# Attention of a hybrid diffusion trunk: score matmuls of two heads in row halves of the array, values stationary in column halves

## The chip, the cores and the metric

One NeuronCore of a Trainium2 chip runs the whole program in one launch. The metric is device time in microseconds (us) from start to end of an execution. Five engines work from queues of their own, each in order: TensorE (PE in the rows, its weight loads PEld), VectorE (DVE), ScalarE (ACT), GpSimd (POOL) and SyncE (SP, which issues most DMAs). They wait for each other through semaphores.

## The reference, cut to what matters

Two layers of a trunk run over 128 context tokens ("ctx") and 512 latent tokens ("lat"). Each layer has a token mixer of three branches (gated linear attention, a short convolution, windowed attention) and a feed-forward part that gathers experts. The change is in the windowed attention alone:

```python
qb = q.reshape(B, nb, ATT_BLOCK, ATT_KV_HEADS, ATT_GROUP, hd)      # 16 heads of 64, 4 key heads
s_loc = jnp.einsum('bnqhgd,bnkhd->bnhgqk', qb, kb) * scale          # 3 key blocks of 128 around each query block
s_loc = jnp.where(valid, s_loc, -jnp.inf)
s_ctx = jnp.einsum('bnqhgd,bchd->bnhgqc', qb, kc) * scale           # 128 cached context keys
m = max(max(s_loc), max(s_ctx), sink)
p_loc, p_ctx = jnp.exp(s_loc - m), jnp.exp(s_ctx - m)
den = sum(p_loc) + sum(p_ctx) + jnp.exp(sink - m)
o = einsum('bnhgqk,bnkhd->bnqhgd', p_loc / den, vb) + einsum('bnhgqc,bchd->bnqhgd', p_ctx / den, vc)
```

Context attention is the same with one block of 128 keys and no mask.

## The kernel before, in words

`attn` works on pairs of heads. A feature tile `ft` (8 per layer) holds two query heads, 64 features each, on the 128 partitions: `qH`, and for the latent tokens `qL`, the rest that the rounded `qH` leaves. Keys are stored the same way, two key heads (`h` = 0, 1) on 128 partitions, but once for each of the two heads with the other head's 64 rows set to zero by `half` (`k_split`, tile `km`, results `kH`, `kL`). So one score matmul contracts over all 128 rows and sees one head. A latent score is three matmuls (`mm3`, lines 198 to 200: H by H, H by L, L by H) into a PSUM tile `S` of the kind `pb` (two buffers) with 3 or 4 blocks of 128 keys, and one or two mask matmuls (L688).

For each block `j` of 128 queries and each head: largest score (L690), its scaled negative `nm` (L691), exponential with row sum (L694) into `P`, transposes of `P` on TensorE (L698) into a `pt` tile, a copy to `PT` (head 0 on DVE, L703; head 1 on ACT, L701, as the flag `FL[0]` is 0), then `P` times `V` (L706) with `PT` as the stationary operand and 64 value columns moving, into `po` with the queries on partitions. After four blocks the sums are inverted, `po` is multiplied by them (L715), and four transposes (L719) turn the tile back to features on partitions; ACT copies it and a DMA stores it (L722).

An fp32 matmul (operands `F32`, as `P`, `V`, the context's scores) is two rows in the trace, an fp32r one (`F32R`, as `qH`, `kH`) or a transpose is one.

Other work shares the queues. In the latent mixer `attn` is a background generator that is advanced while the convolution's projections run (L198 to L200 into `pa`), and the expert gather (POOL fetches, DVE multiplies `gjunk`, `gacc`) advances beside both. In the context mixer it runs beside the merge (L365) and the modulation (L269). A scheduler decides from this at which place in each engine's order an instruction stands.

Two kinds of matmul before the change already use only a part of the array: the modulation (L269) puts 32 weight columns in one of four column groups, and the decay projection (L410) 16 rows at row 0 or row 32.

Of the kernel before, what the change touches and what calls it, by code (L numbers as in the profile page):

```python
# [43 lines left out]
def kernel(ctx: ExitStack, tc: tile.TileContext, A: dict, O: list):  # L44
# [327 lines left out]
    def flat(x):  # L372
        return x.rearrange("p s t -> p (s t)")
# [213 lines left out]
    def attn(s, l, hH, hL, ap):  # L587

        if True:
# [8 lines left out]
            kH = [[t4k([128, nk, 128], "kH%d%d" % (i, h), kt_, s, ap) for h in range(2)] for i in range(2)]  # L598
            kL = [[None if s.ctx else ap.tile([128, nk, 128], F32R, name="kL%d%d" % (i, h), bufs=1)
                   for h in range(2)] for i in range(2)]  # L600

            def k_split(i, pos, x):
                n = x.shape[-1]
# [52 lines left out]
            for un in range(4):  # L656
                ps = proj_fm(s, hH, hL, w_for(s, A["w_in"][l, 24 + un]))
                for f in range(2):
# [12 lines left out]
                    po = po2([128, 2, nq, 64])  # L671
                    for j in range(nq):
# [6 lines left out]
                        n = len(poss)  # L679
                        for h in range(2):  # L680
                            qs = slice(j * 128, (j + 1) * 128)
                            S = pb([128, n, 128])
                            ks = slice(poss[0], poss[0] + n)
                            k2 = lambda x: None if x is None else flat(x[pr][h][:, ks, :])
                            mm3(flat(S), qH[:, qs], None if s.ctx else qL[:, qs], k2(kH),
                                None if s.ctx else k2(kL), True, not masks)
                            for mi, (i, w) in enumerate(masks):
                                nc.tensor.matmul(S[:, i, :], idb, band[:, w, :], start=False, stop=mi == len(masks) - 1)  # L688
                            mx = ap.tile([128, 1], F32, name="mx", bufs=4)
                            V.reduce_max(mx, flat(S), axis=mybir.AxisListType.X)  # L690
                            V.scalar_tensor_tensor(nm[:, j, h:h + 1], mx, -ASCALE, nsink[:, ft, h:h + 1],  # L691
                                                   op0=OP.mult, op1=OP.min)
                            P = ap.tile([128, n, 128], F32, name="P", bufs=2)
                            act(flat(P), flat(S), AF.Exp, scale=ASCALE, bias=nm[:, j, h:h + 1],  # L694
                                accum_out=den[:, j, h:h + 1])
                            ptp = pt([128, n, 128])
                            for i in range(n):
                                nc.tensor.transpose(ptp[:, i, :], P[:, i, :], idf)  # L698
                            PT = ap.tile([128, n, 128], F32, name="PT", bufs=2)
# [18 lines left out]
                    for j in range(nq):  # L718
                        nc.tensor.transpose(p[:, j, :], y[:, j].rearrange("p h d -> p (h d)"), idf)  # L719
# [794 lines left out]
```

## Time and profile before

| | us |
|---|---|
| runs before: median (lowest to highest of 3) | 5597.84 (5595.0 to 5608.46) |
| the profiled execution's own time | 5604.7 |
| its span, first to last instruction | 5602.9 |
| TensorE busy | 5117.3 |
| VectorE busy | 4190.2 |
| ScalarE busy | 2014.7 |
| GpSimd busy | 2482.5 |

Busy times overlap. A busy TensorE is counted from a matmul's start to its modelled end; matmuls are pipelined, so the distance between the starts of two neighbours tells what one costs, not its length. Context attention lies at about 223 to 310 us and 1780 to 1895 us, latent attention at about 720 to 1026 us (layer 0) and 3505 to 3865 us (layer 1).

### The profile page before, as it was taken

To read this page: it belongs to the slowest core of one execution; us is meant where nothing else is said; L and a number is where in the kernel's file an instruction comes from. 1 tells how busy PE (TensorE), PEld (TensorE's weight loads), DVE (VectorE), ACT (ScalarE), POOL (GpSimd) and SP (SyncE) were. 2 spreads that over 40 slices of the span, in tenths; PEclk is the share of its full clock that TensorE was granted. 3 is DMA by queue.
4 is the path that set the end of the run, shared out by engine and by line. 5 is a ranking of instruction groups with operands and counts; after the bars stand their busy time and mean duration, and the time that the engine had idled before them with its cause. 6 is when DMAs were issued, how large, how long until landed. Compare 5 with 4: busy or idle time off the path is not lost. (4 is left out here: it accounts for less than half of the span.)

```text
span 5602.9 us, 78403 instructions
## 1 busy us (share of the span) xinstructions
PE 5117.3 (91%) x28598; PEld 4457.9 (80%) x28598; DVE 4190.2 (75%) x7436; ACT 2014.7 (36%) x3454; POOL 2482.5 (44%) x1907
## 2 busy tenths in 40 slices
PE   8999889988899999899999798998998899999998
PEld 6888777767688998888777587777776899899876
DVE  3328978877544868887777789788878986788777
ACT  2214434221232225653333344333223367333333
POOL 1112434676210006886555543455753254665432
PEclk9999999999899999999999899999998999999999
DMA  7773456887566667899999634578852574999996
GB/s 297 272 246 127 136 185 223 303 297 250 208 222 235 226 233 267 323 337 325 322 314 323 214 123 139 194 257 288 286 187 101 191 260 175 359 324 322 328 327 214
DMA packets 456707, 1395.08 MB, mean 249 GB/s; under 512 B 42880, under 2 KB 184832, under 8 KB 413312
## 3 DMA queue, kind: packets, MB, share of 16 engines
q1 hardware_dynamic: 303248, 833.73, 42.1%
q0 software_dynamic: 153072, 556.34, 28.7%
q8 instruction: 225, 3.69, 0.3%
q14 instruction: 162, 1.33, 0.1%
HBM read 1275.29 MB, written 114.62 MB: 248 GB/s over the span
## 5 line engine op out<-in xcount | busy, mean ns | idle before, releaser
L917 POOL DMA_INDIRECT grow<-in_peer_u_dram,eidx x512 | 696.0, 1359 | 635.6 <-DVE gjunk L922 257.4
L917 POOL DMA_INDIRECT grow<-in_peer_v_dram,eidx x512 | 671.9, 1312 | 553.2 <-DVE gacc L934 248.4
L934 DVE SCALAR_TENSOR_TENSOR gacc<-grow,gw,gacc 128x1024 f32<-128x1024 f32 x508 | 707.0, 1392 | 86.8 <-DMA grow<-in_peer_v_dram,eidx 80.4
L178 POOL TENSOR_TENSOR wl<-wraw,wh 128x640 fp32r<-128x640 f32 (+1 forms) x260 | 413.4, 1592 | 720.5 <-ACT wh L174 659.4
L922 DVE SCALAR_TENSOR_TENSOR gjunk<-grow,gh 128x1024 bf16<-128x1024 f32 x512 | 682.0, 1332 | 67.1 <-DMA grow<-in_peer_u_dram,eidx 62.6
L174 ACT ACTIVATE wh<-wraw 128x1024 fp32r<-128x1024 f32 (+1 forms) x388 | 515.7, 1343 | 520.7 <-PE pa L199 207.3
L176 DVE TENSOR_TENSOR wl<-wraw,wh 128x1408 fp32r<-128x1408 f32 (+2 forms) x388 | 557.5, 1440 | 150.5 <-ACT wh L174 148.2
L198 PE MATMUL acc<-wh,daH 128*128 128x512 f32 x1536 | 611.2, 399 | 51.9 <-ACT daH L112 37.5
L200 PE MATMUL acc<-wh,daL 128*128 128x512 f32 x1536 | 610.7, 398 | 13.8 <-DVE daL L113 13.4
L199 PE MATMUL acc<-wl,daH 128*128 128x512 f32 x1536 | 607.3, 395 | 0.5 <-DVE wl L176 0.5
L198 PE MATMUL pa<-hH,wh 128*128 128x512 f32 x1312 | 542.5, 414 | 43.6 <-DVE th L744 11.2
L200 PE MATMUL pa<-hH,wl 128*128 128x512 f32 x1312 | 535.6, 410 | 9.0 <-DVE wl L176 8.8
L199 PE MATMUL pa<-hL,wh 128*128 128x512 f32 x1312 | 534.8, 408 | 0.5 <-DVE hL L113 0.4
L198 PE MATMUL po<-hH,uH 128*128 128x384 f32 x1376 | 484.3, 352 | 20.6 <-ACT uH L1014 14.0
L200 PE MATMUL po<-hH,uL 128*128 128x384 f32 x1376 | 471.6, 343 | 9.6 <-DVE uL L1016 9.3
L199 PE MATMUL po<-hL,uH 128*128 128x384 f32 x1376 | 470.5, 342 | 0.0
L1014 ACT ACTIVATE uH<-uraw 128x1024 fp32r<-128x1024 f32 x256 | 270.7, 1058 | 555.6 <-PE po L199 223.3
L198 PEld LDWEIGHTS acc<-wh,daH 128*128 128x128 f32 x1536 | 294.4, 192 | 121.7 <-ACT daH L112 47.8
L987 POOL TENSOR_SCALAR ob<-iota,tt,tt 128x128 f32<-128x128 f32 x192 | 292.4, 1528 | 211.0 <-ACT tt L968 91.3
L1016 DVE TENSOR_TENSOR uL<-uraw,uH 128x1024 fp32r<-128x1024 f32 (+1 forms) x256 | 284.4, 1111 | 119.9 <-ACT uH L1014 118.8
L200 PEld LDWEIGHTS acc<-wh,daL 128*128 128x128 f32 x1536 | 293.8, 191 | 91.0 <-DVE daL L113 29.6
L198 PEld LDWEIGHTS pa<-hH,wh 128*128 128x128 f32 x1312 | 255.0, 195 | 110.5 <-DVE th L744 12.9
(367 smaller groups left out, 11610.7 us busy)
## 6 DMA issues: line engine op xcount, KB each, us to landing
wraw<-in_w_in_dram SPq DMA_DIRECT2D x168, 1024.0 KB
uraw<-in_u_T_dram SPq DMA_DIRECT2D x256, 512.0 KB
wraw<-in_v_n_dram SPq DMA_DIRECT2D x256, 512.0 KB
wraw<-in_w_mod_dram SPq DMA_DIRECT2D x48, 1024.0 KB
wraw<-in_w_branch_dram SPq DMA_DIRECT2D x48, 1024.0 KB
gdr<-stage SPq DMA_DIRECT2D x24, 2048.0 KB
G<-gdr SPq DMA_DIRECT2D x64, 768.0 KB
sdr<-ust SPq DMA_DIRECT2D x172, 192.0 KB
```

What stands on the lines that cost most here:

```text
L174: act(H, raw, AF.Copy)
L176: V.tensor_sub(L[:, :m], raw[:, :m], H[:, :m].bitcast(F32))
L178: nc.gpsimd.tensor_sub(L[:, m:], raw[:, m:], H[:, m:].bitcast(F32))
L198: nc.tensor.matmul(out, aH, bH, start=start, stop=False)
L199: nc.tensor.matmul(out, aH, bL, start=False, stop=False)
L200: nc.tensor.matmul(out, aL, bH, start=False, stop=stop)
L917: nc.gpsimd.indirect_dma_start(out=g, out_offset=None, in_=A[tab + str(l)], in_offset=bass.IndirectOffsetOnAxis(ap=eidx[:, j:j + 1], axis=0))
L922: pin(V.scalar_tensor_tensor(junk, g, 1.0, h, op0=OP.mult, op1=OP.mult, accum_out=w[:, j:j + 1]))
L934: pin(V.scalar_tensor_tensor(acc, g, w[:, j:j + 1], acc, op0=OP.mult, op1=OP.add))
L987: (nc.gpsimd if w == "P" else V).tensor_scalar(ob[:, k, :], iota128, TT[1][:, j:j + 1], TT[2][:, j:j + 1], op0=OP.is_equal, op1=OP.mult)
L1014: act(uH, raw, AF.Copy)
L1016: V.tensor_sub(uL[:, :m, :], raw[:, :m, :], uH[:, :m, :].bitcast(F32))
```

## The change

Scores: keys are stored once (no zeroed halves), and each head's score matmul contracts over its own 64 rows, at row 0 or row 64 of the array (`tile_position=(64 * h, 0)`). The two heads' matmuls are issued in turn, into the two `pb` buffers. One `nm` operation serves both heads. Values: `V` (64 columns) is now stationary, in the left or right column half of the array (`tile_position=(0, 64 * h)`), `PT` moves with 128 columns, and `po` comes out with features on partitions. So the closing transposes are gone; instead the reciprocal sums are spread over 64 partitions each by a matmul with the identity (L724 of the changed kernel), copied by ACT to `rd`, and multiplied in. Both heads' `PT` are copied by ACT. The generator yields after the exponentials of both heads and after both heads' `P` times `V`, as many times as before.

```diff
-                for h in range(2):
-                    if s.ctx:
-                        V.tensor_scalar(flat(kH[i][h][:, pos, :]), x, half[:, h:h + 1], None, op0=OP.mult)
-                        continue
-                    km = ap.tile([128, 512], F32, tag="km", name="km", bufs=1)
-                    V.tensor_scalar(km[:, :n], x, half[:, h:h + 1], None, op0=OP.mult)
-                    split(flat(kH[i][h][:, pos, :]), flat(kL[i][h][:, pos, :]), km[:, :n])
+                if s.ctx:
+                    act(flat(kH[i][:, pos, :]), x, AF.Copy)
+                else:
+                    split(flat(kH[i][:, pos, :]), flat(kL[i][:, pos, :]), x)
...
+                        S = [pb([128, n, 128]) for _ in range(2)]
+                        terms = [(qH, kH[pr])] if s.ctx else [(qH, kH[pr]), (qH, kL[pr]), (qL, kH[pr])]
+                        for m, (q_, k_) in enumerate(terms):
+                            for h in range(2):
+                                nc.tensor.matmul(flat(S[h]), q_[hs[h], qs], flat(k_[hs[h], ks, :]), start=m == 0,
+                                                 stop=m == len(terms) - 1 and not masks, tile_position=(64 * h, 0))
...
-                            mm3(flat(S), qH[:, qs], None if s.ctx else qL[:, qs], k2(kH),
-                                None if s.ctx else k2(kL), True, not masks)
...
+                        V.scalar_tensor_tensor(nm[:, j, :], mx, -ASCALE, nsink[:, ft, :], op0=OP.mult, op1=OP.min)
...
-                            if h or FL[0]:
-                                act(flat(PT), flat(ptp), AF.Copy)
-                            else:
-                                V.tensor_copy(flat(PT), flat(ptp))
-                            for i in range(n):
+                            act(flat(PT[h]), flat(ptp), AF.Copy)
+
+                        for i in range(n):
+                            for h in range(2):
                                 vs = slice(pr * 128 + h * 64, pr * 128 + h * 64 + 64)
-                                nc.tensor.matmul(po[:, h, j, :], PT[:, i, :], vt[:, poss[i] % 5, vs],
-                                                 start=i == 0 and j == 0 and h == 0, stop=i == n - 1, skip_group_check=True)
-                            yield
+                                nc.tensor.matmul(po[hs[h], j, :], vt[:, poss[i] % 5, vs], PT[h][:, i, :],
+                                                 start=i == 0 and j == 0, stop=i == n - 1, tile_position=(0, 64 * h),
+                                                 skip_group_check=True)
+                        yield
...
-                        nc.tensor.transpose(p[:, j, :], y[:, j].rearrange("p h d -> p (h d)"), idf)
-                    yT = ap.tile([128, nq, 128], F32, name="yatT", bufs=1)
-                    act(flat(yT), flat(p), AF.Copy)
+                        for h in range(2):
+                            nc.tensor.matmul(p[hs[h], j, :], den[:, j, h:h + 1].to_broadcast([128, 64]), idf,
+                                             start=True, stop=True, tile_position=(0, 64 * h), skip_group_check=True)
+                    rd = ap.tile([128, nq, 128], F32, name="rd", bufs=1)
+                    act(flat(rd), flat(p), AF.Copy)
+                    yT = ap.tile([128, nq, 128], F32, name="yatT", bufs=2)
+                    V.tensor_mul(flat(yT), flat(po), flat(rd))
```

First place: TensorE's order in latent attention of layer 0, at the scores of a query block of four key blocks. Before, the scores of the two heads (`kH00`, `kH01`: the same keys with one or the other half zeroed) stand together behind a run of `P` times `V`:

```order
L706 MATMUL po_6574<-vt_5576,PT_6629 128x64 x4
L706 MATMUL po_6574<-vt_5576,PT_6651 128x64 x4
L198 MATMUL pb_6733<-kH01_5569,qH_6560 128x512
L199 MATMUL pb_6711<-kL00_5572,qH_6560 128x512
L199 MATMUL pb_6733<-kL01_5573,qH_6560 128x512
L200 MATMUL pb_6711<-kH00_5568,qL_6561 128x512
L200 MATMUL pb_6733<-kH01_5569,qL_6561 128x512
```

Now (L684, row halves; `pb_6240` is head 0, `pb_6241` head 1) transposes of the previous block's `P` (L704, full array) stand between them:

```order
L704 MATMUL pt_6218<-idf_75,P_6214 128x128
L684 MATMUL pb_6240<-kH0_5556,qH_6106 128x512
L704 MATMUL pt_6218<-idf_75,P_6214 128x128
L684 MATMUL pb_6240<-kL0_5558,qH_6106 128x512
L684 MATMUL pb_6241<-kH0_5556,qH_6106 128x512
L704 MATMUL pt_6218<-idf_75,P_6214 128x128
L684 MATMUL pb_6241<-kL0_5558,qH_6106 128x512
L704 MATMUL pt_6218<-idf_75,P_6214 128x128
L684 MATMUL pb_6240<-kH0_5556,qL_6107 128x512
L684 MATMUL pb_6241<-kH0_5556,qL_6107 128x512
```

What moved: the six score matmuls are as many as before, but full-array and row-half instructions now alternate.

Second place: TensorE's order at `P` times `V` in the same stretch. Before (L706, all on the full array, as the transposes L698 and the scores of the next block are):

```order
L706 MATMUL po<-vt,PT 128x64 x4
L698 MATMUL pt<-idf,P 128x128 x4
L706 MATMUL po<-vt,PT 128x64 x2
L698 MATMUL pt<-idf,P 128x128 x4
L198 MATMUL pb<-kH_5568,qH 128x512
```

Now (L711 and the spreading of the reciprocal sums L724 in column halves; L704, and the convolution's L198 to L200, on the full array):

```order
L711 MATMUL po<-PT,vt 64x128
L198 MATMUL pa<-hH,wh 128x512
L199 MATMUL pa<-hL,wh 128x512
L200 MATMUL pa<-hH,wl 128x512
L711 MATMUL po<-PT,vt 64x128 x7
L704 MATMUL pt<-idf,P 128x128 x3
L198 MATMUL pa<-hH,wh 128x512
L199 MATMUL pa<-hL,wh 128x512
L704 MATMUL pt<-idf,P 128x128 x2
L724 MATMUL pt<-idf,den 64x128 x2
L704 MATMUL pt<-idf,P 128x128
L724 MATMUL pt<-idf,den 64x128 x2
```

What moved: one or two column-half matmuls stand alone between others, seven stand together, and the spreading has come in between.

Third place: VectorE's order in latent attention of layer 0. Before:

```order
L690 TENSOR_REDUCE mx<-pb 128x1 x2
L691 SCALAR_TENSOR_TENSOR nm<-mx,nsink 128x1
L703 COPY PT<-pt 128x384
L691 SCALAR_TENSOR_TENSOR nm<-mx,nsink 128x1
L922 SCALAR_TENSOR_TENSOR gjunk,gw<-grow,gh 128x1024
L703 COPY PT<-pt 128x512
```

Now (`gacc` is a row of the expert gather):

```order
L692 TENSOR_REDUCE mx<-pb 128x1 x2
L942 SCALAR_TENSOR_TENSOR gacc<-grow,gw,gacc 128x1024
L693 SCALAR_TENSOR_TENSOR nm<-mx,nsink 128x2
L582 TENSOR_TENSOR yc<-yc,pa 128x512
L942 SCALAR_TENSOR_TENSOR gacc<-grow,gw,gacc 128x1024
L176 TENSOR_TENSOR wl<-wraw,wh 128x1408
```

What moved: the copies to `PT` are gone from this queue (they are on ACT), and one `nm` of both heads follows both largest scores.

## Rows read from the trace of the kernel before

**Rows 1.** The page, part 1: busy us, share of the span, instructions of each engine.
```profile
PE 5117.3 (91%) x28598; PEld 4457.9 (80%) x28598; DVE 4190.2 (75%) x7436; ACT 2014.7 (36%) x3454; POOL 2482.5 (44%) x1907
```

**Rows 2.** Table by stage: the four attention stretches; then clock, DMA share, GB/s.
```profile
core 0 of [0], span 5602.9 us
...
223.00:310.00 87.00, 85.64 (x669) 76.41 (x670) 23.11 (x93) 19.55 (x82) 16.99 (x17) 1.00 0.85 305
1780.00:1895.00 115.00, 114.69 (x838) 104.51 (x838) 62.68 (x282) 30.19 (x102) 2.98 (x1) 1.00 0.65 226
720.00:1026.00 306.00, 294.86 (x1714) 240.66 (x1713) 260.45 (x432) 122.21 (x241) 137.01 (x116) 0.99 0.65 214
3505.00:3865.00 360.00, 326.94 (x1809) 266.33 (x1807) 299.18 (x481) 130.55 (x251) 176.98 (x144) 0.95 0.69 232
```

**Rows 3.** Groups by line, 720 to 1026 us: busy us, mean ns | idle before.
```profile
L706 PE MATMUL po<-vt,PT 128*128 128x64 f32 x448 | 57.5, 269 | 0.5 <-DVE PT L703 0.4
L706 PEld LDWEIGHTS po<-vt,PT 128*128 128x128 f32 x448 | 56.8, 191 | 5.9 <-ACT PT L701 1.9 <-DVE PT L703 1.4 <-issue 0.5
...
L703 DVE COPY PT<-pt 128x384 f32<-128x384 f32 (+1 forms) x32 | 19.8, 618 | 3.8 <-PE pt L698 3.3 <-PE po L706 0.2
...
L691 DVE SCALAR_TENSOR_TENSOR nm<-mx,nsink 128x1 f32<-128x1 f32 x64 | 14.8, 233 | 0.0
...
L719 PE MATMUL pt<-idf,yat 128*128 128x128 f32 x32 | 4.8, 273 | 0.0
```

**Rows 4.** Timeline, 783 to 805 us: start, us, engine, instruction, count.
```profile
783.24 0.39 PE L199 MATMUL pb<-kL,qH 128*128 128x512 f32 x1
783.47 0.40 PE L200 MATMUL pb<-kH,qL 128*128 128x512 f32 x1
...
784.06 0.75 PEld L706 LDWEIGHTS po<-vt,PT 128*128 128x128 f32 x6
...
795.90 0.34 PE L199 MATMUL pb<-kL,qH 128*128 128x384 f32 x1
796.07 0.34 PE L200 MATMUL pb<-kH,qL 128*128 128x384 f32 x1
...
803.62 0.60 PE L719 MATMUL pt<-idf,yat 128*128 128x128 f32 x4
```

**Rows 5.** Timeline around a change of the array's shape, 232 to 238 us.
```profile
232.83 3.12 PE L365 MATMUL pa<-yH,wraw 128*128 128x128 f32 x26
235.88 0.14 PEld L269 LDWEIGHTS pb<-wraw,cT 128*32 128x32 f32 x2
235.88 0.62 PE L269 MATMUL pb<-wraw,cT 128*32 128x256 f32 x2
...
236.43 0.30 PEld L196 LDWEIGHTS pb<-kH,qH 128*128 128x128 f32 x2 [0.41 <-issue]
...
236.85 0.58 PEld L269 LDWEIGHTS pb<-wraw,cT 128*32 128x32 f32 x14
...
237.84 0.74 PEld L365 LDWEIGHTS pa<-hF,wraw 128*128 128x128 f32 x6 [0.41 <-issue]
```

**Rows 6.** Line L269: durations in ns, least, median, most.
```profile
L269 PE MATMUL pb<-wraw,cT x768: 379/379/637, 8.8 to 1865.0; 128*32 128x256 f32 x192
```

**Rows 7.** Timeline: one 16-row group at 84 us, two at 98 us.
```profile
83.92 0.48 PE L410 MATMUL pb<-gaT,a 16*128 16x128 f32 x2
...
84.34 0.41 PEld L365 LDWEIGHTS pa<-hF,wraw 128*128 128x128 f32 x3
...
97.61 0.49 PE L410 MATMUL pb<-gaT,a 16*128 16x128 f32 x4
...
98.03 0.63 PEld L365 LDWEIGHTS pa<-hF,wraw 128*128 128x128 f32 x5
```

**Rows 8.** Who waited for whom, PE, 3505 to 3865 us: total, times, longest.
```profile
PE pb L198 <- ACT qH L112: 8.2, 3, 5.5
PE pa L200 <- DVE wl L176: 6.8, 3, 4.8
```

More of the change, by code (lines that the diff above doesn't have):

```diff
@@ L597, in attn @@
             kt_ = F32 if s.ctx else F32R
-            kH = [[t4k([128, nk, 128], "kH%d%d" % (i, h), kt_, s, ap) for h in range(2)] for i in range(2)]
-            kL = [[None if s.ctx else ap.tile([128, nk, 128], F32R, name="kL%d%d" % (i, h), bufs=1)
-                   for h in range(2)] for i in range(2)]
+            kH = [t4k([128, nk, 128], "kH%d" % i, kt_, s, ap) for i in range(2)]
+            kL = [None if s.ctx else ap.tile([128, nk, 128], F32R, name="kL%d" % i, bufs=1) for i in range(2)]
             def k_split(i, pos, x):
-                n = x.shape[-1]
-                for h in range(2):
-                    if s.ctx:
-                        V.tensor_scalar(flat(kH[i][h][:, pos, :]), x, half[:, h:h + 1], None, op0=OP.mult)
-                        continue
-                    km = ap.tile([128, 512], F32, tag="km", name="km", bufs=1)
-                    V.tensor_scalar(km[:, :n], x, half[:, h:h + 1], None, op0=OP.mult)
-                    split(flat(kH[i][h][:, pos, :]), flat(kL[i][h][:, pos, :]), km[:, :n])
+                if s.ctx:
+                    act(flat(kH[i][:, pos, :]), x, AF.Copy)
+                else:
+                    split(flat(kH[i][:, pos, :]), flat(kL[i][:, pos, :]), x)
             vt = ap.tile([128, 1 if s.ctx else 5, 256], F32, name="vt", bufs=1)
@@ L679, in attn @@
                         n = len(poss)
-                        for h in range(2):
[L681 to L684, printed above, removed]
-                            mm3(flat(S), qH[:, qs], None if s.ctx else qL[:, qs], k2(kH),
-                                None if s.ctx else k2(kL), True, not masks)
[L687 to L694, printed above, removed]
@@ new lines, in attn @@
+                        qs = slice(j * 128, (j + 1) * 128)
+                        ks = slice(poss[0], poss[0] + n)
+                        hs = [slice(64 * h, 64 * h + 64) for h in range(2)]
+                        S = [pb([128, n, 128]) for _ in range(2)]
[4 more added lines that the diff above has]
+                                                 stop=m == len(terms) - 1 and not masks, tile_position=(64 * h, 0))
@@ new lines, in attn @@
+                        for mi, (i, w) in enumerate(masks):
+                            for h in range(2):
+                                nc.tensor.matmul(S[h][:, i, :], idb, band[:, w, :], start=False,
+                                                 stop=mi == len(masks) - 1)
+                        mx = ap.tile([128, 2], F32, name="mx", bufs=4)
+                        for h in range(2):
+                            V.reduce_max(mx[:, h:h + 1], flat(S[h]), axis=mybir.AxisListType.X)
+                        V.scalar_tensor_tensor(nm[:, j, :], mx, -ASCALE, nsink[:, ft, :], op0=OP.mult, op1=OP.min)
@@ L695, in attn @@
+                        P = []
+                        for h in range(2):
+                            P.append(ap.tile([128, n, 128], F32, name="P", bufs=2))
+                            act(flat(P[h]), flat(S[h]), AF.Exp, scale=ASCALE, bias=nm[:, j, h:h + 1],
                                 accum_out=den[:, j, h:h + 1])
+                        yield
+                        PT = []
+                        for h in range(2):
                             ptp = pt([128, n, 128])
                             for i in range(n):
-                                nc.tensor.transpose(ptp[:, i, :], P[:, i, :], idf)
@@ L709, in attn @@
+                        yield
                     es = ap.tile([128, nq, 2], F32, name="es", bufs=2)
```

10 lines of the change are left out of this document (5 added, 5 removed).

## Prediction

> **What bounds the kernel now.** I read the page first, to see which engine the span is made of. TensorE (PE) has work for 91% of it [rows 1], so the question is whether PE is also what the four attention stretches wait for. The table by stage answers that [rows 2]: context attention (223 to 310 us, 1780 to 1895 us) has PE busy 85.6 of 87 and 114.7 of 115 us; latent attention has it busy 294.9 of 306 us in layer 0 and 326.9 of 360 us in layer 1. VectorE (DVE) stands at 260 of 306 us, ScalarE (ACT) at 122. So in three stretches time is the sum of what PE's queue holds; only in the fourth are there 33 us to fill, and 11 in the second, 44 together. The longest PE waits of that fourth stretch are for qH and wl [rows 8], made by ACT and DVE.
>
> PE executes its queue in order, so I take the change as a sum over PE's instructions, multiplied by distances between neighbours in the trace.
>
> **What the array is given less of.** Per latent layer, before: 192 score matmuls, half of 384 and half of 512 columns, start 0.17 and 0.23 us apart [rows 4], mean 0.20: 38.4 us. 448 rows of P times V (224 matmuls, two rows each [rows 3]), whose weight loads follow each other at (0.75-0.19)/5 = 0.112 us [rows 4] (one lasts 0.19 [rows 3]): 50.2 us. 32 closing transposes at (0.60-0.27)/3 = 0.11 us [rows 4] (one lasts 0.27 [rows 3]): 3.5 us. Together 92.1 us.
>
> Do halves of the array run side by side? The trace of before has both kinds. The modulation matmul (L269) uses four column groups: alone in its group the second row of a pair starts 0.62-0.38 = 0.24 us after the first (0.38 is the length of one [rows 6]), while 14 of them take 237.84-236.85 = 0.99 us, 0.07 each [rows 5]. The decay matmul (L410) uses 16-row groups: from its start to the next weight load of the full array one group's two rows take 84.34-83.92 = 0.42 us, and two groups' four rows 98.03-97.61 = 0.42 us [rows 7]. So I take two halves for the price of one, where the order puts both halves next to each other. It often does not: counted over the order of the changed kernel, 56 of the 192 score matmuls of a latent layer stand without a partner (a transposition of P is between them, as in the first place shown above), so 68+56 = 124 slots of 0.20: 24.8 us. Of 288 column-half matmuls (224 of P times V, 64 that spread the reciprocal sums) 58 have none: 115+58 = 173 slots of two rows at 0.11: 38.1 us. After: 62.9 us, 29.2 less per latent layer. The 224 transposes of P, the masks and the rotary matmuls stay. Context attention, by the same counting with 128-column fp32 scores (0.22 each): 8.1 us before, 7.5 and 7.7 after. All four: 2 x 29.2 + 1.0 = 59.4 us less.
>
> **What it is given more of: changes of the array's shape.** The changed kernel goes from full to row halves to column halves and back. Before, the order has 166 such changes (L269 and L410); after, 915: 749 more, 653 of them in latent attention (342 and 311). Their price is in [rows 5]. The 26 rows of L365 start (3.12-0.27)/25 = 0.114 apart (0.27 as for L706 and L719 [rows 3]); the last starts at 235.68 and has streamed at 235.79, but the first weight load of the column groups begins at 235.88: 0.09 us in which nothing starts. Then L196: from its load (236.43) to the next group's (236.85) are 0.42 us: two streams of 0.114, again 0.09 of standing, and 0.10 in which the array waits for the first 128 columns of weights, which nothing hides. So 0.20 us where full-width fp32 weights or score weights come next (213 to scores, 101 to other full ones, latent; 67 in context): 381 x 0.20 = 76.2. I take 0.15 where 64-column weights or transposes come next (half the load to hide; a choice between 0.09 and 0.20): 136+159 latent, 29 context: 324 x 0.15 = 48.6; 0.12 for 44 masks: 5.3. Sum 130.1 us. Bounds: 749 x 0.09 = 67 and 749 x 0.20 = 150.
>
> Here a rule of the Trainium skill speaks against the change. TensorEngine Tiling (Array Packing), section Key Properties: changing the tiling mode, as against the tile, drains TensorE. It gives no time; if a drain lasted until the recorded end of the last matmul (0.27 us after its start, 0.16 after its stream), a switch would cost 0.07 us more than the rows show and the sum would rise by some 50 us. The rows show 0.09, and I go by them.
>
> **Moved off and onto the other engines.** DVE loses 32 copies of turned probabilities per latent layer (19.8 us [rows 3]) and half of 64 small scalings of 0.233 us (7.4 us), besides the masked key halves: some 30 of 260 busy us. ACT takes the copies (about the same 0.6 us each): 122 to about 142 of 306 us, still far from full. The cover for ACT is PE's bound. The closing multiply stays one DVE operation per tile, and one PSUM copy on ACT remains. What the lighter DVE gives is that waits of PE for DVE's products shrink: of 44 us of PE idle [rows 2] I take 10; bounds 0 and 44. The number of DMAs is unchanged: the same one store per feature tile.
>
> **Sum.** 130.1 - 59.4 - 10 = +60.7 us. The profiled execution took 5604.7 us (span 5602.9 [rows 2]), so 5665; it stands 6.9 us over the median of the runs (5597.84), in whose terms I forecast **5658 us**.
>
> **Rivals.**
> - *The switch is free* (ends on the other side). If what the halves load is fetched while the full array still streams, 749 changes cost nothing and 59.4 us are gained: 5538 us. It decides at 59.4/749 = 0.079 us a switch: below that the kernel is faster. Against it: [rows 5] shows 0.09 of standing three times in a row, before any weight. For it: those are 32-wide groups, and no row shows 64-wide ones. 7%. The Trainium skill (TensorE: Matmul & The Clock Gate, Part 3, The mechanism) has weight loads pulled ahead of running matmuls where row groups differ; a half and the full array share theirs.
> - *PE's idle time swallows it.* If a lighter DVE and a busier PE use up all 44 us, +27 remain: 5625. For it: the waits in [rows 8] are for DVE's and ACT's work. Against: in layer 0 there are only 11 us to use, and ACT's products are as late as before. 15%.
> - *The halves do not overlap* (64 rows of fp32r, or 64 columns, one after the other). Scores take 192 slots and not 124 (13.6 us), column halves 288 and not 173 (25.3 us), per layer 39, both 78, with context some 80: 5738. Against it: [rows 5, 7]. 8%.
> - *A new wait takes over.* Both heads' turned probabilities are now copied on ACT one behind the other, and P times V of the second head waits for it: 64 times about 0.6 us (one copy, [rows 3]) if nothing else is in the queue: +38, 5696. Against: between the copies and the use the order has other matmuls. 10%.
>
> **How the numbers follow.** My forecast has 60%, its own range 5635 to 5690 (switches at 0.16 to 0.20, idle 0 to 20). About 0.3%, some 17 us, is what a measurement of this kernel can tell from no change. Faster: the free switch, 7%. Same (up to 5615): the low end of swallowed idle time and a switch at its bound of 0.09, which together give 67-59-10, no change: 8%. Slower: the rest, 85%. For 8 in 10 the range leaves out the free switch, and halves that never overlap: 5606 to 5705 us.
>
> **What would show it.** In the changed profile: score rows of two heads starting a few ns apart where they stand in pairs; 0.09 us or more between the end of a stream and the next weight load at each change of shape; L706's 448 rows replaced by as many whose pairs share their time; latent stretches some 25 to 35 us longer in layer 0, less in layer 1, context 7 to 9 us each; DVE about 30 us less busy per latent stretch and this not shown in the span. I am wrong if the standing at a switch is under 0.08 us, if PE idles longer than 44 us in the latent stretches, or if the granted clock there, now 0.99 and 0.95, falls.

## The result: one per cent slower, at 5661 us

The changed kernel takes 5661.44 us (median of 4 runs, 5655.83 to 5664.42), the kernel before 5602.43 us on the same chip (4 runs, 5595.0 to 5608.46). The ratio is 1.010, 95% interval 1.0079 to 1.0121: 59 us slower. The forecast was 5658 us. The profiled execution took 5658.53 us, its span is 5656.8 us, 53.9 more than that of [rows 1, 2].

The page of the changed kernel, part 1, in the columns of [rows 1]:

```profile
PE 5176.3 (92%) x28838; PEld 4411.0 (78%) x28838; DVE 4124.8 (73%) x7232; ACT 2047.3 (36%) x3526; POOL 2493.5 (44%) x1907
```

PE is busy for 59 us more, DVE for 65 us less, and the span grows nearly as PE's time does. For the stages I cut both traces at the same events: context attention from the fetch of the sinks (`nsink`) to the first `wo` of the merge, latent attention from that fetch to the first matmul on `yH`. The table by stage of the changed kernel, with the columns of [rows 2] (us, PE, PEld, DVE, ACT, POOL, clock, DMA share, GB/s):

```profile
217.50:375.30 157.80, 152.11 (x1168) 135.83 (x1169) 23.77 (x88) 26.39 (x109) 24.08 (x33) 0.98 0.79 284
728.80:1074.60 345.80, 331.04 (x1853) 225.74 (x1853) 240.75 (x365) 140.29 (x274) 148.60 (x122) 0.97 0.61 203
1805.90:2040.20 234.30, 234.25 (x1663) 215.58 (x1663) 156.78 (x570) 55.62 (x154) 12.86 (x21) 1.00 0.62 223
3550.20:3915.10 364.90, 341.94 (x1910) 235.51 (x1909) 283.85 (x410) 146.03 (x279) 190.12 (x152) 0.96 0.71 240
```

And the same cut through the trace before:

```profile
215.60:361.10 145.50, 142.63 (x1145) 132.02 (x1144) 26.53 (x108) 23.99 (x99) 24.12 (x33) 1.00 0.85 308
711.30:1034.60 323.30, 304.70 (x1756) 248.97 (x1756) 268.59 (x444) 127.11 (x248) 143.97 (x121) 0.98 0.65 216
1771.70:1998.10 226.40, 226.09 (x1638) 213.96 (x1637) 160.80 (x590) 52.77 (x144) 13.42 (x21) 1.00 0.65 229
3504.50:3862.40 357.90, 326.97 (x1811) 266.55 (x1809) 299.18 (x481) 129.32 (x249) 176.98 (x144) 0.95 0.69 230
```

The reader is to see four lengths: +12.3, +22.5, +7.9 and +7.0 us, 49.7 of the 53.9. In the two latent stretches the second and third numbers of a row, length and PE's busy time, split this further. PE's busy time, which I call its work below, grew by 26.3 us in layer 0 (304.7 to 331.0) and by 15.0 in layer 1 (327.0 to 341.9). PE's idle time, the rest of the length, fell from 18.6 to 14.8 and from 30.9 to 23.0. Part of it is one wait at the very end, in which PE has run out of attention and convolution and waits for `yH`, the operand of the merge: 7.3 us in layer 0 and 0.1 in layer 1 before, 7.4 and 11.3 after. In layer 1 the row that ends the stretch is, before and changed:

```profile
3862.37 0.50 PE L198 MATMUL pa<-yH,wh 128*128 128x512 f32 x1
```

```profile
3915.12 1.22 PE L198 MATMUL pa<-yH,wh 128*128 128x512 f32 x2 [11.29 <-ACT yH L112]
```

So layer 1 lost only 7.0 us for two reasons: its work grew less, and the idle time ahead of this last wait fell by 19, of which 11 came back at the end. (The expectations of the later runs leave the last wait out: their 43 us of idle time before and 20 after stand for 42.1 and 19.1 here, the rest lies just ahead of the stretch.)

The granted clock was 0.98 and 0.95 before, 0.97 and 0.96 after. By the clock rows of the two traces PE worked at the lower level (1.2 GHz) for 8.9 and 30.2 us before, and for 13.5 and 17.1 after. A 512-column matmul stands 0.43 us from the next there (before, 3625.30 to 3625.73 us) and 0.23 at the upper level. From these numbers I estimate that the clock added 2 us of work in layer 0 and took 6 off in layer 1, so at one clock the work grew by some 24 and 21 us.

What the new instructions do is in the timeline of the changed kernel around 810 us, the first place that the text on the change shows (start, us, engine, instruction):

```profile
810.07 0.40 PE L200 MATMUL pa<-hH,wl 128*128 128x512 f32 x1
...
810.30 0.27 PE L704 MATMUL pt<-idf,P 128*128 128x128 f32 x1
...
810.50 0.18 PEld L684 LDWEIGHTS pb<-kH,qH 64*128 64x128 f32 x1 [0.20 <-PE pa L200]
810.50 0.50 PE L684 MATMUL pb<-kH,qH 64*128 64x512 f32 x1
...
810.93 0.33 PE L704 MATMUL pt<-idf,P 128*128 128x128 f32 x1
...
811.19 0.18 PEld L684 LDWEIGHTS pb<-kL,qH 64*128 64x128 f32 x1
811.19 0.50 PE L684 MATMUL pb<-kL,qH 64*128 64x512 f32 x1
811.19 0.18 PEld L684 LDWEIGHTS pb<-kH,qH 64*128 64x128 f32 x1
811.19 0.49 PE L684 MATMUL pb<-kH,qH 64*128 64x512 f32 x1
...
811.62 0.33 PE L704 MATMUL pt<-idf,P 128*128 128x128 f32 x1
```

Two heads' scores start together at 811.19, their weight loads too, and the pair costs 0.43 us (811.19 to 811.62). But a score alone in its half costs the same 0.43 (810.50 to 810.93), where a full-array score of 512 columns stood 0.23 from the next [rows 4]. And each transpose between them costs 0.26 (810.93 to 811.19) where it cost 0.11. The transpose at 810.30 has streamed its 128 columns at 810.41; the next load begins at 810.50. So a pair of scores inside this alternation gains nothing, a lone one loses 0.20, and each transpose, whose work nobody changed, loses 0.15.

The array stands as long ahead of column halves. From the last full-array row of 512 columns to the first `P` times `V` it is 0.33 us, 0.10 more than the 0.23 from one such row to the next:

```profile
829.75 0.40 PE L200 MATMUL pa<-hH,wl 128*128 128x512 f32 x1
...
830.08 0.85 PEld L711 LDWEIGHTS po<-PT,vt 128*64 128x64 f32 x14 [0.37 <-issue]
```

Groups by line for latent layer 0 of the changed kernel (728.8 to 1074.6 us), with the columns of [rows 3]:

```profile
L704 PE MATMUL pt<-idf,P 128*128 128x128 f32 x224 | 54.0, 300 | 1.3 <-ACT P L697 1.3
L711 PE MATMUL po<-PT,vt 128*64 128x128 f32 x448 | 46.8, 286 | 0.2
...
L706 ACT ACTIVATE PT<-pt 128x384 f32<-128x384 f32 (+1 forms) x64 | 34.5, 544 | 65.1 <-PE pt L704 61.4 <-PE pb L688 3.6
...
L724 PE MATMUL pt<-idf,den 128*64 128x128 f32 x128 | 11.5, 282 | 0.0
...
L693 DVE SCALAR_TENSOR_TENSOR nm<-mx,nsink 128x2 f32<-128x2 f32 x32 | 4.9, 154 | 0.3
```

Busy times hide it, since pipelined matmuls overlap. Summed from each start to the next start on PE, less idle time, layer 0 gives (us):

| | before | changed |
|---|---|---|
| transposes of P | 22.5 | 39.9 |
| scores | 43.2 | 47.5 |
| P times V | 46.2 | 40.1 |
| closing transposes, or spreading of the sums | 2.9 | 9.0 |
| masks and rotary matmuls | 11.6 | 13.9 |
| projections beside them | 177.9 | 180.8 |

The sum is +26.9, where the busy time grew by 26.3. Two thirds of it stand at the transposes of P.

### The profile page after: what moved, and what is told of

Read it like the earlier page. It is cut to its first block, busy times and chain, and to the rows that moved or that the text cites. A ratio compares the mean times of both kernels' runs of the same rounds, so it can differ in the third digit from the quotient of the medians.

```text
span 5656.8 us, 78839 instructions
## 1 busy us (share of the span) xinstructions
PE 5176.3 (92%) x28838; PEld 4411.0 (78%) x28838; DVE 4124.8 (73%) x7232; ACT 2047.3 (36%) x3526; POOL 2493.5 (44%) x1907
## 5 line engine op out<-in xcount | busy, mean ns | idle before, releaser
L198 PE MATMUL acc<-wh,daH 128*128 128x512 f32 x1536 | 610.4, 398 | 58.7 <-ACT daH L112 41.8
L200 PE MATMUL acc<-wh,daL 128*128 128x512 f32 x1536 | 610.7, 398 | 13.7 <-DVE daL L113 13.6
L198 PE MATMUL pa<-hH,wh 128*128 128x512 f32 x1312 | 542.3, 414 | 36.8 <-DVE th L752 12.6
L200 PE MATMUL pa<-hH,wl 128*128 128x512 f32 x1312 | 532.8, 407 | 1.5 <-DVE wl L176 1.5
L198 PE MATMUL po<-hH,uH 128*128 128x384 f32 x1376 | 484.8, 352 | 18.1 <-ACT uH L1022 11.6
L200 PE MATMUL po<-hH,uL 128*128 128x384 f32 x1376 | 470.7, 342 | 9.6 <-DVE uL L1024 9.4
L198 PEld LDWEIGHTS acc<-wh,daH 128*128 128x128 f32 x1536 | 294.2, 192 | 128.9 <-ACT daH L112 53.1
L200 PEld LDWEIGHTS acc<-wh,daL 128*128 128x128 f32 x1536 | 293.5, 191 | 90.8 <-DVE daL L113 30.3
L199 PEld LDWEIGHTS acc<-wl,daH 128*128 128x128 f32 x1536 | 293.8, 191 | 60.6 <-DVE wl L176 1.0
```

Source lines behind the costliest of these rows:

```text
L198: nc.tensor.matmul(out, aH, bH, start=start, stop=False)
L199: nc.tensor.matmul(out, aH, bL, start=False, stop=False)
L200: nc.tensor.matmul(out, aL, bH, start=False, stop=stop)
```

## The experiments

The theory: 749 more changes of the array's shape cost 0.15 to 0.20 us each, lone halves gain nothing, and the halves' gain is smaller. The rivals: a change is nearly free and the loss is waits for ScalarE and the new order; or the loss comes from PE's idle time. All ratios are to the kernel before, run beside each group on the same chip (medians 5611.97 us for e1 to e4, 5606.01 for e5 to e8, 5611.68 for e9 to e12). Each row on work and idle time is one trace; in brackets is the last wait, for `yH`, which is part of the idle time.

| kernel | changes of shape | median us | ratio, 95% | latent 0: PE work + idle (last wait) | latent 1 |
|---|---|---|---|---|---|
| before | 166 |  |  | 304.7 + 18.6 (7.3) | 327.0 + 30.9 (0.1) |
| changed | 915 | 5661.44 | 1.010, 1.0079 to 1.0121 | 331.0 + 14.8 (7.4) | 341.9 + 23.0 (11.3) |
| e1_full_array | 166 | 5655.13 | 1.0076, 1.0059 to 1.0093 | 320.1 + 16.8 (2.7) | 339.8 + 32.1 (6.9) |
| e2_cols_only | 492 | 5625.52 | 1.0025, 1.0015 to 1.0035 | 309.4 + 17.6 (7.3) | 324.1 + 27.3 (11.3) |
| e3_rows_only | 637 | 5647.28 | 1.0059, 1.0042 to 1.0076 | 334.1 + 18.9 (10.8) | 341.9 + 29.3 (15.8) |
| e4_grouped | 553 | 5605.46 | 0.9991, 0.9981 to 1.0000 | 295.8 + 30.4 (10.3) | 302.1 + 36.9 (10.2) |
| e5_price_one | 368 | 5634.75 | 1.0051, 1.0035 to 1.0067 | 322.6 + 17.6 (8.4) | 344.0 + 27.5 (0.0) |
| e6_price_two | 566 | 5666.69 | 1.0107, 1.0090 to 1.0123 | 335.2 + 17.4 (7.9) | 353.2 + 29.2 (0.0) |
| e7_cols_grouped | 352 | 5602.48 | 0.9989, 0.9979 to 1.0000 | 298.8 + 22.3 (8.1) | 312.1 + 34.6 (11.6) |
| e8_grouped_shared | 550 | 5601.41 | 0.9986, 0.9972 to 0.9999 | 289.9 + 34.2 (13.7) | 309.8 + 32.8 (8.2) |
| e9_before_copies_act | 166 | 5594.5 | 0.9981, 0.9971 to 0.9991 | 308.5 + 18.0 (7.4) | 320.6 + 17.6 (5.9) |
| e10_grouped_bufs | 553 | 5607.57 | 1.0000, 0.9989 to 1.0011 | 295.8 + 28.5 (8.6) | 299.9 + 37.5 (10.1) |
| e11_copies_shared | 874 | 5672.56 | 1.0112, 1.0096 to 1.0128 | 334.9 + 24.9 (7.8) | 332.2 + 22.0 (11.3) |
| e12_changed_again | 915 | 5650.19 (one run) | | 330.7 + 14.7 (6.8) | 340.0 + 23.1 (9.9) |

### One part of the change at a time

Scores, P times V and the spreading of the sums on the full array, in the changed kernel's code (e1; the scores there see both heads, `V` and the sums 128 columns, so the instructions are as many and none has a partner; the edit of the sums is not shown):

```diff
-nc.tensor.matmul(flat(S[h]), q_[hs[h], qs], flat(k_[hs[h], ks, :]), ..., tile_position=(64 * h, 0))
+nc.tensor.matmul(flat(S[h]), q_[:, qs], flat(k_[:, ks, :]), ...)
...
-nc.tensor.matmul(po[hs[h], j, :], vt[:, poss[i] % 5, vs], PT[h][:, i, :], ..., tile_position=(0, 64 * h), ...)
+nc.tensor.matmul(po[:, j, :], vt[:, poss[i] % 5, pr * 128:pr * 128 + 128], PT[h][:, i, :], ...)
```

> The changed kernel with its code order, its copies and its waits, but every attention matmul on the full array: scores contract over all 128 rows (the two heads' scores are added up), values of both heads are stationary in 128 columns (both heads' sums are mixed), reciprocal sums spread over 128 rows. So there are no changes of the array's shape beyond the 166 of the kernel before, and no two halves side by side. Switch theory: the 749 switches (130 us) are gone, the shared time of the halves is gone too: scores 84 us, column work 640 x 0.22 = 141 us, 225 us of streams against 200 before, so about 15 us over the kernel before (+5 to +30), some 45 us under the changed kernel. Wait theory (the longer chain for two heads, all copies on ScalarE): the same chain and more streams, so no faster than the changed kernel: +55 to +85 over before.

Column halves alone (e2: keys zeroed and full-array scores, as in the kernel before; the edit of the keys is not shown):

```diff
-nc.tensor.matmul(flat(S[h]), q_[hs[h], qs], flat(k_[hs[h], ks, :]), ..., tile_position=(64 * h, 0))
+nc.tensor.matmul(flat(S[h]), q_[:, qs], flat(k_[h][:, ks, :]), ...)
```

> The changed kernel with the scores of before (keys with one half zeroed, full array), values and reciprocal sums in column halves as changed. The order has 492 switches, 326 more than before. Switch theory: streams 31 us less than before, 326 switches at 0.15 to 0.18 are 49 to 59 us, 5 us of idle time given back: +13 to +25 over the kernel before. Wait theory: the chain and the copies are those of the changed kernel, so +50 or more.

Row halves alone (e3: P times V and the closing as in the kernel before; the edit of the closing is not shown):

```diff
-nc.tensor.matmul(po[hs[h], j, :], vt[:, poss[i] % 5, vs], PT[h][:, i, :], ..., tile_position=(0, 64 * h), ...)
+nc.tensor.matmul(po[:, h, j, :], PT[h][:, i, :], vt[:, poss[i] % 5, vs], ...)
```

> The changed kernel with its scores in row halves, but P times V and the closing transposes as before (full array, probabilities stationary); all copies on ScalarE as changed. The order has 637 switches, 471 more than before. Switch theory: streams 28 us less than before, 471 switches at 0.17 to 0.20 are 80 to 94 us, 10 us of idle time given back: +40 to +58 over the kernel before, most of the loss in the rows and not in the columns. Wait theory: +50 or more here too, and as much as in the kernel with columns alone.

The columns cost 14 us, the rows 35: e2 is where the switch theory put it, e3 5 us under its range, and the rows are where the loss is. e2 can also be set directly against the changed kernel, for PE's queue holds the same rows in the same order but for 40 of 28838 places: row halves instead of full-array scores are 381 more changes of shape in latent attention (653 against 272) and 39.5 us more of PE's work (673.0 against 633.5). With the 27 us that the prediction gives the shared slots of the scores (2 x 13.6), a change there costs (39.5 + 27.2)/381 = 0.175 us, or 0.155 with the clock taken out as above.

e1 came out at +43, a miss for the switch theory (its range ended at +30) and for the wait theory alike. PE's latent work in it grew by 15.4 and 12.8 us (12 expected in each) without a single new change of shape, so this part held. The rest was not foreseen: its latent idle time stayed at 48.9 us, where the changed kernel has 37.8, and of the 51.9 us that its trace is longer, 13.2 lie in context attention and 11.2 outside of attention. The code is the changed kernel's, but PE's queue is not (another row at 2540 of 28838 places), so e1 does not tell what the changed order costs. This run alone would not have told the causes apart; the next two do.

### The price of a change of shape by itself

In the kernel before, a head's keys are zero in the other head's 64 rows. So a score matmul may read only its own 64 rows and compute the same. PE's order of instructions is the same, row for row (all 28598 in both traces):

```diff
-mm3(flat(S), qH[:, qs], None if s.ctx else qL[:, qs], k2(kH),
-    None if s.ctx else k2(kL), True, not masks)
+terms = [(qH, kH)] if s.ctx else [(qH, kH), (qH, kL), (qL, kH)]
+for m, (q_, k_) in enumerate(terms):
+    hf = not s.ctx and m in (1,)        # e6: (0, 2)
+    r = slice(64 * h, 64 * h + 64) if hf else slice(0, 128)
+    nc.tensor.matmul(flat(S), q_[r, qs], flat(k_[pr][h][r, ks, :]), ..., tile_position=(64 * h, 0) if hf else None)
```

> The kernel before, with every instruction at its old place, in which the second of the three score matmuls of a latent head reads only that head's 64 rows of the array (the other 64 rows multiply zeros in the kernel before, so nothing computed changes). By the order this is 202 more changes of shape (166 to 368) for the same columns; 27 of the 128 halves come next to one of the other head and may share their time (27 x 0.20 = 5 us less). Theory 'a change of shape stops the array, 0.09 us of standing plus up to 0.10 of weight load that nothing hides': 202 x 0.15 to 0.20 - 5 = +25 to +35 us, with some of it in PE's idle time: +20 to +35. Only the standing, 0.09: +13. Rival 'the loss of the changed kernel is waits for ScalarE and the order, a switch is free': -5 to 0.

> As the last one, with the first and third of the three score matmuls of a latent head in the head's 64 rows, the second on the whole array: 400 more changes of shape (166 to 566), 56 of the 256 halves next to another (up to 11 us less). Theory 'each change costs 0.15 to 0.20': 60 to 80 - 11 = +49 to +69 us, less what PE's idle time takes: +35 to +65, about twice that of the run with 202. Only the standing, 0.09: +25. Rival 'a switch is free': -11 to 0.

Measured: +28.7 and +60.7 us in medians, both inside what the switch theory gave and twice as much for twice the switches; a free switch is out. With the halves that have a partner taken at 0.20 us each, a change costs (28.7 + 5)/202 = 0.167 and (60.7 + 11)/400 = 0.179 us; the intervals of the two ratios allow 0.12 to 0.21 and 0.15 to 0.20. In layer 0 of e5 the scores went from 43.2 to 60.2 us and every other kind stayed within 0.8. Timeline of e5_price_one, one head's three scores and its masks:

```profile
763.75 0.48 PE L689 MATMUL pb<-kH,qH 128*128 128x512 f32 x1
...
764.16 0.18 PEld L689 LDWEIGHTS pb<-kL,qH 64*128 64x128 f32 x1 [0.25 <-issue]
764.16 0.50 PE L689 MATMUL pb<-kL,qH 64*128 64x512 f32 x1
764.59 0.19 PEld L689 LDWEIGHTS pb<-kH,qL 128*128 128x128 f32 x1 [0.25 <-issue]
764.59 0.50 PE L689 MATMUL pb<-kH,qL 128*128 128x512 f32 x1
...
764.92 0.29 PE L693 MATMUL pb<-band,idb 128*128 128x128 bf16 x2
```

The kernel before, the same kind of place:

```profile
760.19 0.47 PE L198 MATMUL pb<-kH,qH 128*128 128x512 f32 x1
...
760.27 0.19 PEld L199 LDWEIGHTS pb<-kL,qH 128*128 128x128 f32 x1
...
760.50 0.40 PE L199 MATMUL pb<-kL,qH 128*128 128x512 f32 x1
...
760.73 0.39 PE L200 MATMUL pb<-kH,qL 128*128 128x512 f32 x1
...
760.97 0.29 PE L688 MATMUL pb<-band,idb 128*128 128x128 bf16 x2
```

Before, the weights of the second score are loaded (760.27) under the matmul ahead of it, 0.23 before its own start. After a change of shape the load begins with the matmul (764.16 twice, 764.59 twice). From the first score to the masks it is 0.78 us before and 1.17 here: 0.39 for two changes.

### Fewer changes by another order

e4 has the changed kernel's instructions, kept in groups on PE: scores wait until the block's transposes are through, column halves follow each other, the head whose copy comes last goes first, and the sums are spread after the last P times V.

```diff
-                            for h in range(2):
+                            for h in (1, 0):
-                                nc.tensor.matmul(flat(S[h]), q_[hs[h], qs], ...)
+                                i_ = nc.tensor.matmul(flat(S[h]), q_[hs[h], qs], ...)
+                                if lastT[0]:
+                                    behind(i_, lastT[0])
...
```

> The changed kernel, all of its arithmetic, with order constraints on TensorE alone: a block's scores come behind the previous block's transposes of P, the head whose inputs are ready later is issued first of its pair, and the spreading of the sums comes behind the last P times V. The order has 553 switches where the changed kernel has 915, and fewer halves without a partner (54 where it has 272). Switch theory: 362 switches of 0.17 less (62 us) and 23 us of streams less than the changed kernel: about 85 us under it, 25 us under the kernel before (5540 to 5600 in the terms of before's 5600). Wait theory: the constraints only add waits, so no faster than the changed kernel.

In the timeline of e4_grouped a whole block now is one run of each kind:

```profile
806.48 0.50 PE L685 MATMUL pb<-kH,qH 64*128 64x512 f32 x2
806.82 0.40 PE L685 MATMUL pb<-kL,qH 64*128 64x512 f32 x2
807.05 0.40 PE L685 MATMUL pb<-kH,qL 64*128 64x512 f32 x2
807.38 0.40 PE L691 MATMUL pb<-band,idb 128*128 128x128 bf16 x4
807.71 1.09 PE L715 MATMUL po<-PT,vt 128*64 128x128 f32 x16
...
808.73 0.50 PE L200 MATMUL pa<-hH,wl 128*128 128x512 f32 x1
```

Six scores take 0.90 us (806.48 to 807.38), where six of the full array took 1.38 at 0.23 each, and sixteen rows of P times V 1.02 where they took 1.79 at 0.112. That is the gain that the halves can give. PE's work fell 8.9 and 24.9 us under the kernel before, with 362 switches and 218 lone halves fewer than in the changed kernel. By the ratios (1.010 less 0.9991, of 5605) e4 is 61 us faster than the changed kernel, but only 6 us under the kernel before (the interval ends at 1.0), where the switch theory gave some 25, because PE now idles 67 us in latent attention, 18 more than before. Of these, 20.5 are the last waits for `yH` (10.3 and 10.2). Who it waited for ahead of that in latent layer 1 of e4_grouped (total, times, longest):

```profile
PE pt L707 <- ACT P L700: 9.1, 9, 1.9
PE pa L198 <- ACT rx L633: 6.2, 2, 3.8
PE pb L685 <- ACT qH L112: 3.5, 3, 1.5
```

Three attempts at that rest. Full-array scores with grouped column halves (e7, e2 with the grouping of the second kind only):

```diff
                         for i in range(n):
-                            for h in range(2):
+                            for h in (1, 0):
...
-                            nc.tensor.matmul(p[hs[h], j, :], den[:, j, h:h + 1].to_broadcast([128, 64]), idf, ...)
+                            i_ = nc.tensor.matmul(p[hs[h], j, :], den[:, j, h:h + 1].to_broadcast([128, 64]), idf, ...)
+                            behind(i_, lastV)
```

> The changed kernel with scores on the full array (as in e2_cols_only) and the column halves set close together: per step of a tile the head whose copy comes last goes first, and the spreading of the reciprocal sums waits for the last P times V. By the order 352 changes of shape and 8 unpaired column halves, where e2_cols_only has 492 and 134. Theory 'switches and unpaired halves': 140 x 0.15 = 21 us and 126 x 0.11 = 14 us less than e2_cols_only (+13.5): -21 us against the kernel before, or down to 0 if PE's idle time takes up what PE's queue loses, as it did in e4_grouped. Rival 'the order of the heads and ScalarE's copies cost it': it stays at e2_cols_only's +13 or above.

e4 with the first head's copy on DVE (e8):

```diff
-                            act(flat(PT[h]), flat(ptp), AF.Copy)
+                            if h:
+                                act(flat(PT[h]), flat(ptp), AF.Copy)
+                            else:
+                                V.tensor_copy(flat(PT[h]), flat(ptp))
```

> e4_grouped with the copy of the first head's turned probabilities back on VectorE, as in the kernel before. In e4_grouped PE idles 48 us in the latent stretches, most of it for ScalarE's P (14 us), qH (13) and yH (20). Theory 'PE's queue got shorter by 21 us and ScalarE, which carries all copies, sets what comes instead': -10 to -25 us against the kernel before, where e4_grouped has -6. Rival 'the idle time is the order's, not ScalarE's load': within 5 us of e4_grouped, -11 to 0. By the new-wait rival of the prediction (copies one behind the other on ScalarE) it would be 30 us or more under e4_grouped.

e4 with four buffers for `P` and `PT` instead of two (e10):

```diff
-P.append(ap.tile([128, n, 128], F32, name="P", bufs=2))
+P.append(ap.tile([128, n, 128], F32, name="P", bufs=4))
-PT.append(ap.tile([128, n, 128], F32, name="PT", bufs=2))
+PT.append(ap.tile([128, n, 128], F32, name="PT", bufs=4))
```

> e4_grouped with four buffers instead of two for the probabilities and four for the turned ones; the order of the work is the same. If PE's 48 us of idle time there come from buffers that are not free yet: -15 to -30 us against the kernel before. If they come from the chain from scores over softmax to transposes in this order: as e4_grouped, -6, within 6.

e7's grouping took 17 us off e2, but ended at -3.5 us, near the idle-time end of its range. e8 and e10 idle 67 and 66 us, as e4 does with 67: neither the first head's copy nor the number of these buffers is the limit. What is left is the chain from scores over softmax to transposes in this order, which no run changed alone. (The 48 us of e4 in the expectation of e8 leave out the `yH` of the list that it gives.) e8's -5 us is within 5 of e4's -6.5.

### ScalarE's copies and PE's idle time

The kernel before with one flag changed (e9):

```diff
-    FL = (0, 1, 0, 1)
+    FL = (1, 1, 0, 1)
```

> The kernel before, with the first head's copies of the turned probabilities on ScalarE too, where the changed kernel has them; 32 copies (19.8 us) per latent layer go from VectorE to ScalarE, and the order of the work shifts with them. The prediction's term 'a lighter VectorE takes 10 us of PE's 44 us of idle time': -5 to -20 us against the kernel before, PE idle in the latent stretches some 33 us. If it was VectorE's load that the changed kernel got rid of (it idles 20): -20. Rival 'idle time depends on the order, not on VectorE's load': 0, within 8 us, idle still near 44. Rival 'copies one behind the other on ScalarE are a new wait': +20 to +38.

The changed kernel with the first head's copy back on DVE (e11, the edit of e8):

> The changed kernel with the first head's copy of turned probabilities back on VectorE; 874 changes of shape instead of 915. Theory 'changes of shape and unpaired halves': 41 x 0.17 = 7 us less, 46 more or fewer unpaired halves give back some of it: +35 to +55 against the kernel before (the changed kernel: +59). Rival 'copies one behind the other on ScalarE are the new wait': 38 less, +15 to +25. If VectorE's lighter load is what cut PE's idle time from 43 to 20 us, the idle time comes back and the run is at +60 to +75.

And the changed kernel again, without an edit:

> The changed kernel once more, for PE's idle time in the latent stretches alone: 20 us if the 20 of the first trace are its own, up to 40 if an execution decides it.

e9 is 11 us faster than the kernel before by its ratio (0.9981, 0.9971 to 0.9991; 17 between medians), the lowest ratio of these runs, and so beats both kernels. Its trace flatters it: that execution took 5582.15 us, the shortest of nine, 12 under their median. The table by stage of e9_before_copies_act, latent layer 1:

```profile
3504.20:3842.30 338.10, 320.55 (x1815) 259.19 (x1814) 286.55 (x454) 148.68 (x285) 190.02 (x147) 0.98 0.72 250
```

Its PE waits there:

```profile
PE pa L198 <- ACT yH L112: 5.9, 1, 5.9
PE pb L200 <- DVE qL L113: 2.7, 2, 2.0
...
PE pb L198 <- ACT qH L112: 2.3, 2, 1.2
...
PE pa L200 <- DVE wl L176: 0.9, 2, 0.6
```

The waits of 8.2 us for `qH` and 6.8 for `wl` [rows 8] are 2.3 and 0.9 here. PE's idle time in layer 1 fell from 30.9 to 17.6 us with all matmuls on the full array, and the granted clock rose from 0.95 to 0.98; layer 0 gained nothing (323.3 to 326.5 us). But the copies' move also changed the order: PE's queue holds another row than before at 2127 of 28598 places. So e9 shows what the move is worth with the order that came with it, and not whether VectorE's lighter load or the order took the idle time away. The same waits in layer 1 of the changed kernel:

```profile
PE pt L704 <- ACT P L697: 4.0, 4, 2.4
PE pa L198 <- ACT rx L632: 2.3, 1, 2.3
PE pb L684 <- ACT qH L112: 2.2, 2, 1.2
```

No wait for `PT` (L706) is among them. e11 gives the copies back to DVE and is no faster: +61 us by medians, over the range of the switch theory (+55), far from the +25 or less of the copies as a new wait, and where the third branch put it. That branch's reason is borne out in part only: its trace, the longest of four, idles 46.9 us, 9 more than the changed kernel, where 23 had been expected back.

e12's one run idles 37.8 us in the latent stretches, as the first trace of the changed kernel does, so this idle time is the kernel's own. It took 5650.19 us, 38.5 over the median of the kernel before beside it and 6 under the lowest of the four runs at the top; one run is too little to set against their 59.

## Why the prediction was right, and what was mis-sized

**Changes of shape: +130 predicted.** Right in place, and near in price. The standing is 0.09 us at every kind of change in the trace after (810.41 to 810.50 above): at the upper clock the next shape starts 0.20 us after a 128-column row of the full array, of row halves, of column halves or of 16 rows, where the next row of the same shape starts after 0.11. A score that follows a change costs 0.20 more, a transpose 0.15, as taken. e5 and e6 give 0.167 and 0.179 all told, which times 749 is 125 to 134. The page TensorEngine Tiling (Array Packing) of the Trainium skill, Key Properties, says that a change of mode drains TensorE. The runs agree in that no load starts for 0.09 us, but the array does not wait for the recorded end of the matmul: the transpose of 810.30 is recorded to 810.57 (0.27 long), and the next load begins at 810.50.

**Halves: -59 predicted.** Pairs share their time (811.19 above) and lone ones gain nothing, as the counting of slots has it. With the switches in latent attention priced at 112 us and the halves' 58 taken off, PE's work there was to grow by 54; it grew by 41.3. This is the term that was mis-sized, by 13 us. By the estimate above 4 of them are the clock, which stood lower before than after in layer 1. The other 9 are in the price, the slots or both: with the slots as counted the price would be (41.3 + 4 + 58)/653 = 0.158 us and not 0.172. No run separates the two.

**Idle time: -10 predicted.** 49.5 us became 37.8, so 11.7 were taken in. The nearness is luck. Ahead of the last wait 23 us were taken in (42.1 to 19.1), more than twice the term, and 11 came back as the wait for `yH` at the end of layer 1, which the prediction did not look for: its window of layer 0 ends at 1026 us, ahead of the 7.3 us that PE waits there. All kernels with the changed code have such a wait in layer 1, of 7 to 16 us; e5 and e6, in the order of the kernel before, have none. The rival that all of the idle time goes was half true for the part that it counted.

**Context attention: 7 to 9 us each.** The second gave 7.9, the first 12.3. In the first, 2.8 of it is idle time, and the clock stood at 0.98 of 1.00, up to 3.2 us of 157.8; I had looked for neither.

**Latent stretches: 25 to 35 us longer in layer 0, less in layer 1.** They are 22.5 and 7.0 longer: the order is right, layer 0 just under the range. The last sign of being wrong, a lower clock, came in layer 0 (0.98 to 0.97 in the same cut) and not in layer 1. The other two did not come: the standing is 0.09 us, and PE idles 37.8 us in the latent stretches, not over 44.

**VectorE some 30 us lighter per latent stretch.** 27.8 in layer 0, 15.3 in layer 1. PE's waits for DVE's and ACT's products ahead of the last one shrank as predicted, only more; that the lighter DVE is the cause is not shown (e9 above).

**The sum.** Predicted +60.7 on the profiled execution, found +53.9 there and +59.0 between medians. On the trace, 13 us less of latent work and 2 more of idle time taken in stand against 4 more in context attention and 4 outside attention, where nothing had been forecast. So the forecast is right by its mechanism and its main terms, and that it lies within 4 us of the median (5658 and 5661) is in part luck: errors of either sign cancel, and the medians are 5 us further apart than the two traces. Halves and switches without the copies' move make, by the two ratios, 1.010 less 0.9981 of 5605, 67 us, where 130.1 - 59.4 = 70.7 was worked out; this takes it that the two parts add up, which no run shows, and the intervals (12 and 6 us to either side) are wider than the difference.

**The rivals.** The free switch falls with e5 and e6. Halves that do not overlap fall with the rows at 811.19 and with e4's six scores in 0.90 us. The new wait for copies on ScalarE falls with the waits, with e11, and with e9, where both copies stand on ScalarE and the kernel is faster.

**Open.** Why e1 keeps 49 us of idle time and the grouped kernels e4, e8 and e10 idle 66 to 67, where the changed kernel idles 38. Their longest waits name `yH`, `P` and `qH`, products of ScalarE, which suggests that the order decides how long the chain through the softmax is covered; no run changed the chain alone. Open too is whether e9's gain comes from VectorE's load or from the order that changed with it.

## What to carry to other kernels

Halving the array's use pays only if halves stand next to each other in pairs and in runs: count the changes of shape in PE's order, multiply by the measured price (0.17 us here) and set that against the slots that pairs save. Here an order of groups won the whole loss back (61 us) with the same instructions. When a change bundles an engine move with a reshaping, run the move alone: here it made the kernel before faster by 0.2%, which the bundle hid. And when a stretch is cut at an event, see what the engine did just before that event: a wait there is idle time too.

## What the runs showed of the hardware

Two 64-row halves load their weights at the same time (both at 811.19, 0.18 us each, as long as a full one of 0.19) and start within the same 0.01 us. A change from full array to row halves, to column halves and back leaves the same 0.09 us, so no kind of change was cheap. And PE's idle time did not take in the price of switches: in e5 and e6 PE's work in the latent stretches grew by 35 and 57 us and its idle time only went from 49.5 to 45 and 47, so in these two runs added work on PE did not simply fill the waits that were there.
